# A two-layer decoder trunk on one core: a pool for layer 0's residual halves, more buffers in layer 1's attention, and spatial gating two groups to a PSUM bank

## The chip, the core and the metric

The kernel runs on one core of one Trainium2 chip. The metric is device time in microseconds (us) of one execution; the time before is the median of three runs, 2185.39 us (2182.7 to 2185.51). A core has a matrix engine (TensorE, PE in the profile; its weight loads are shown as PEld), VectorE (DVE), ScalarE (ACT), GpSimd (POOL) and SyncE (SP). Every DMA of this kernel is issued from SP's queue, in order: an issue that has to wait for something holds up the issues behind it. Matrix results land in PSUM, eight banks of 128 partitions by 512 f32 numbers; everything else stands in SBUF, 128 partitions wide.

## The reference

The input is one sequence of 1024 tokens with 1024 features, and two layers follow. Every layer is a mixer and a gated MLP, each added to the residual. Cut to what the change touches:

```python
# layer 0, mixer A: spatial gating, 8 groups of 64 columns, chunks of 128 tokens
vn = layer_norm(gelu(v), ln_g, ln_b)                 # (chunks, 128, 8, 64)
mixed = einsum('gts,bnsgc->bntgc', tril(w_s), vn) + b_s.T[:, :, None]
a_out = gelu(u) * mixed
# mixer B: dilated sliding-window attention, three branches mixed by their log-denominators -> b_out
x = x + concat([a_out, b_out]) @ w_out               # out_proj of layer 0
x = x + conv_ffn(rms_norm(x), ...)

# layer 1: gated linear attention, 4 heads, q, k 128 wide, v 256 wide
attn = where(causal, q_t @ k_t.T, 0)
o = attn @ v + q_t @ state                           # state = decay * (state + k.T @ v), chunk by chunk
o = rms_norm(o, head_g) * silu(r)
x = x + o @ w_out
x = x + conv_ffn(rms_norm(x), ...)
```

## The kernel before

Tokens are cut into eight tiles of 128 (n = 0 to 7). Products run in a split format: a number is a rounded high part and a low part (`split`, L98 to L101, one cast on ACT and one subtraction on DVE), and three matmuls (`PASSES`) give one product. The Tile framework has a planner that takes the traced program, simulates it, and fixes the order of the instructions on each engine and of the DMA issues on SP; it also places each pool's tiles. A pool is an area of SBUF or PSUM with so many buffers for each tag; pools are stacked from the left or from the right end, and an area that an earlier pool used is taken over tile by tile (`reuse_waits="tile"`): a new tile waits for the release of the old tiles that lay at its place, and of no others.

Layer 0's mixer (`even`) has five PSUM pools, opened in the order pt (2 banks), sc (2), pj (2), po (1), tq (1). `project` and `dilated` run pair after pair of heads: scores go to sc, the transposes of the probabilities to pt, the projection to pj. `gmlp` (L587) follows. `proj512` makes one v tile per n in a pj bank; after four of them `consume` normalises the half on DVE (L612 to L619) and does spatial gating: for each of eight groups g one plain f32 matmul (L623) of `ws[:, g]` with 64 columns of four token tiles, 256 columns in all, into a bank of sc, and one DVE eviction (L624) that adds the group's bias and writes over the input columns in `mx`. `u_proj` (L630) then makes the u tiles and multiplies them into `mx` (L635). The planner runs gating beside the u matmuls.

The out_proj comes in two halves of 512 output columns. `out_first` (L432) does the first: `prep(n)` loads the tile `cat` (from `bcat` in layer 0, from `ogd` in layer 1; L1140, L1145) and `xh`, the residual half (L438), transposes eight blocks into two banks of pt (`pc`, L442) and splits them into `hq`; `out_half` (L426) accumulates 24 matmuls (`po`), adds them into `xh` (L429) and writes `xh` to `xd` (L430). After the third tile `first_sides` (L214) makes weight sums for the MLP in the tags qr, qS and qw and writes them out. These PSUM tiles stand in pools mm (3) and pt (2), opened when `even` has closed its own. `out_second` (L456) does the other half in pairs of tiles: `xt` is loaded from `xd` and `x` (L497, L498), 24 matmuls are added (L429) and written out (L430), and `norm` (L144) takes the square sum on ACT (L148), the inverse root on POOL (L140, L141), scales `xt` in place on DVE (L152) and transposes it (L162).

Layer 1 (`gla`, L837): `values` (L881) makes v (L906) and writes it to `vsd`. For each head h two streams (q with k, and r; L990) run, and `core` (L1038) goes through eight chunks n: it loads a chunk of v (L1043), multiplies k and q (`pat`, L1046), turns k (L1049), copies it on ACT (`kt`, L1051), makes the chunk's k-v product (L1052), masks on DVE (L1054), adds state and chunk products into `pog` (L1056, L1057), updates the state (L1061 to L1065), takes the square sum on ACT into `og` (L1068), scales into `og` on DVE (L1070) and writes it to `ogd` (L1071). Layer 1's `out_first` gates the transposes (L1157) with `silu(r)` (L1105) before it splits them.

In the SBUF map of the compiled kernel before, op0 takes 28 KB a partition on the right, just under `gm` (the gating's tiles), with its tags from the bottom in the order cat (2 x 2 KB), xh (2 x 2), qr (2 x 4), qS (2 x 2), qw (2 x 4). The 8 KB of the first `xt` pair begin 1.5 KB above the bottom of op0.

Of the kernel before, what the change touches and what calls it, by code (L numbers as in the profile page):

```python
# [9 lines left out]
F32 = mybir.dt.float32  # L10
# [4 lines left out]
ALU = mybir.AluOpType  # L15
# [4 lines left out]
P = 128  # L20
# [6 lines left out]
GROUPS = 8  # L27
# [28 lines left out]
def trunk(ctx: ExitStack, tc: tile.TileContext, a, out):  # L56
    nc = tc.nc
    V, A, G, T, Q = nc.vector, nc.scalar, nc.gpsimd, nc.tensor, nc.sync
# [370 lines left out]
        V.tensor_add(xh, xh, pd)  # L429
        Q.dma_start(xd[l][n][:, half * 512 : half * 512 + 512], xh)  # L430

    def out_first(l, get_cat, w, x_in, ps, pool, between, gated=None):  # L432

        def prep(n):
            c = get_cat(n)
            gate = gated and gated(n)
            xh = pool.tile([P, 512], F32, tag="xh", name=f"xh{n}")
            Q.dma_start(xh, x_in(n)[:, :512])  # L438
            for g in range(2):
                pt = ps.tile([P, 4, P], F32, tag="pt", name=f"pc{n}{g}")  # L440
                for j in range(4):
                    T.transpose(pt[:, j, :], c(2 * j + g), ident)  # L442
                dst = [hq[g][n // 4][:, i, :, (n % 4) * P : (n % 4 + 1) * P] for i in range(2)]
                split(dst, gate(g, pt) if gated else pt)
            return xh

        xh = [prep(n) for n in range(AHEAD)]
        wo = load_half(w[0], "wo0")
        for n in range(NT):
            if n + AHEAD < NT:  # L450
                xh.append(prep(n + AHEAD))
            out_half(l, 0, wo, n, ps, xh[n], "m1" if l else "mm")
            if n == 2:
                between()
# [132 lines left out]
    def gmlp(ps, gm):  # L587

        wv = load_half(a["w_vu"][0], "wv", g0)
        lnG = gm.tile([P, 512], F32, name="lnG")  # L590
        Q.dma_start(lnG, a["ln_g"].partition_broadcast(P))
        lnB = gm.tile([P, 512], F32, name="lnB")
        Q.dma_start(lnB, a["ln_b"].partition_broadcast(P))
        bs = gm.tile([P, GROUPS], F32, name="bs")
        Q.dma_start(bs, a["a_bs"])
        ws = gm.tile([P, GROUPS, P], F32, name="ws")
        Q.dma_start(ws, a["a_ws"])

        G.affine_select(out=ws, in_=ws, compare_op=ALU.is_ge, fill=0.0, base=0,
                        pattern=[[0, GROUPS], [1, P]], channel_multiplier=-1)  # L600

        def consume(n, pj):
            half, j = n // 4, n % 4
            A.activation(mx[half][:, j, :], pj, AF.Copy, scale=r0[:, n : n + 1])
            if j < 3:
                return
            ge = A.activation(flat(mx[half]), flat(mx[half]), AF.Gelu)
            if half:
                tc.keep_in_program_order(ge)
            for j in range(4):  # L610
                gv = mx[half][:, j, :]
                st = small.tile([P, 6], F32, tag="bn", name=f"bn{half}{j}")  # L612
                V.bn_stats(st, gv)
                mv = small.tile([P, 2], F32, tag="mv", name=f"mv{half}{j}")
                V.bn_aggr(mv, st)
                r = inv_rms(mv[:, 1:2], 1, 1, f"lr{half}{j}")
                V.tensor_scalar(gv, gv, mv[:, 0:1], r, op0=ALU.subtract, op1=ALU.mult)
                V.tensor_mul(gv, gv, lnG)
                V.tensor_add(gv, gv, lnB)  # L619
            for g in range(GROUPS):  # L620
                gc = mx[half][:, :, g * 64 : g * 64 + 64]
                pm = ps.tile([P, 4, 64], F32, tag="sc", name=f"pm{half}{g}")
                T.matmul(pm, ws[:, g, :], gc, start=True, stop=True)  # L623
                V.tensor_scalar(gc, pm, bs[:, g : g + 1], None, op0=ALU.add)  # L624

        mx = [gm.tile([P, 4, 512], F32, name=f"mx{h}") for h in range(2)]
        proj512(ps, wv, "pv", consume)
        return [mx[n // 4][:, n % 4, :] for n in range(NT)]

# [201 lines left out]
    def odd(ps, narrow, rl):  # L831

        with tc.tile_pool(name="T", bufs=1, reuse_waits="tile") as tp, \
                tc.tile_pool(name="gl", bufs=2, reuse_waits="tile") as gl:
            return gla(ps, narrow, gl, [tp.tile([P, 2, 4, 512], F32R, name=f"Tm{i}") for i in range(3)], rl)

    def gla(ps, narrow, gl, T3, rl):  # L837
        right = {1: hq[0][0], 2: hq[1][0], 3: hq[1][1], 4: hq[0][1], 5: T3[0], 6: T3[1], 7: T3[2]}
# [42 lines left out]
        def values():  # L881

            for i, (col, step, w) in enumerate(((0, 272, 1), (256, 256, 2), (512, 512, 1))):
                if i == 0:
                    wv = [w_ for k in range(4) for w_ in load_w(a["w_v0"][k], f"wv0{k}", 272)]
                elif i == 1:
                    wv = [w_ for k in range(2) for w_ in load_w(a["w_v1"][k], f"wv1{k}")]
                else:
                    wv = load_half(a["w_v23"], "wv2")
                for m in sorted(range(NT // (2 * w)), key=lambda m: 2 * w * m < 4):  # L890
                    pv = ps.tile([P, 2, 512], F32, tag="mm", name=f"pv{i}{m}")
                    for j in range(2 * w):
                        n = 2 * w * m + j
                        mm_tok([(pv[:, j // w, (j % w) * 256 : (j % w) * 256 + step], slice(0, step))],
                               lambda k: tok(n, k),
                               lambda k: at(wv, k // 2, (k % 2) * step, step) if i == 1 else wv[k], KD)
                    end = gl.tile([P, 2, S], F32, tag="out", name="vend", bufs=1) if (i, m) == (2, 1) else None
                    for j in range(2):
                        n = w * (2 * m + j)
                        if end is not None:  # L900
                            v = end[:, j, :512]
                        elif i == 0:
                            v = gl.tile([P, 256], F32, tag="v", name=f"v{i}{n}", bufs=3)
                        else:
                            v = gl.tile([P, 512], F32, tag="s1", name=f"v{i}{n}", bufs=1)
                        A.copy(v, pv[:, j, : v.shape[-1]])  # L906
                        c = v.shape[-1] // w
                        Q.dma_start(vsd.rearrange("(n p) c -> p n c", p=P)[:, n : n + w, col : col + c],
                                    v.rearrange("p (n c) -> p n c", c=c))
                    if i == 0:  # L910
                        ns = slice(2 * m, 2 * m + 2)
                        split([gae[:, ns, 0:16], gae[:, ns, 32:48]], pv[:, :, 256:272])
                        V.tensor_copy(gae[:, ns, 64:80], f32(gae[:, ns, 0:16]))
                    if i:
                        if 2 * (i - 1) + m in [1, 0, 4, 5]:
                            three_sides([1, 0, 4, 5].index(2 * (i - 1) + m))
                    if (i, m) == (1, 1):
                        decay_input()
                    if (i, m) == (2, 2):
                        first = decays(0, "mm")  # L920
            return first
# [116 lines left out]
        def core(h, q, k, dec):  # L1038
            st = None
            for n in range(NT):  # L1040
                ts_ = slice(n * P, n * P + P)
                v = gl.tile([P, 256], F32, tag="v", name=f"v{h}{n}", bufs=3)
                Q.dma_start(v, vsd[ts_, h * 256 : h * 256 + 256])  # L1043
                three = ps.tile([P, 512], F32, tag="pt", name=f"pat{h}{n}")
                pat, pkt, pkv = three[:, :P], three[:, P : 2 * P], three[:, 2 * P :]
# [12 lines left out]
                if n < NT - 1:  # L1058
# [4 lines left out]
                        V.tensor_add(new, st, pkv)  # L1063
                    st = new
                    V.tensor_scalar(st, st, dec[:, n : n + 1], None, op0=ALU.mult)  # L1065
                og = gl.tile([P, 256], F32, tag="og", name=f"og{h}{n}")
                ssq = small.tile([P, 1], F32, tag="ssq", name=f"oss{h}{n}")
                A.activation(og, po, AF.Square, accum_out=ssq)  # L1068
                r = inv_rms(ssq, 1, 256, f"ro{h}{n}")
# [4 lines left out]
        ps = narrow()  # L1074
# [54 lines left out]
    ps = banks(pss, mm=3, pt=2)  # L1129
    for l in range(2):  # L1130
        w_out = a["od_w_out" if l else "ev_w_out"]
        x_in = (lambda n: x2[n]) if l else (lambda n: rows(a["x"], n))
        with ExitStack() as ops:
            if l == 1:
                ps, last = odd(ps, narrow, ops.enter_context(tc.tile_pool(name="rl", bufs=1, side="right", reuse_waits="tile")))
            pool = ops.enter_context(tc.tile_pool(name=f"op{l}", bufs=2, side="left" if l else "right", reuse_waits="tile"))

            def cat0(n):
# [20 lines left out]

                return gate  # L1160

            out_first(l, cat1 if l else cat0, w_out, x_in, ps, pool, lambda: first_sides(l, pool, 2), gated if l else None)
        gms.close()
        with tc.tile_pool(name=f"T{l}", bufs=1, reuse_waits="tile") as tp:
            T3 = [tp.tile([P, 2, 4, 512], F32R, name=f"T{l}{i}") for i in range(3)]
            if l == 0:
                ps = narrow()
# [4 lines left out]
        ps = banks(pss, mm=3, pt=2)  # L1172
        with ExitStack() as st:
            pool = st.enter_context(tc.tile_pool(name=f"fd{l}", bufs=1, reuse_waits="tile"))
# [103 lines left out]
```

## Time and profile before

| what | value |
|---|---|
| median of the three runs | 2185.39 us |
| profiled execution | 2186.67 us, of which the span from first to last instruction is 2185.0 us |
| PE busy | 2145.9 us, 98% of the span |
| DVE, ACT, POOL busy | 1538.2, 1032.7, 488.4 us |
| mean granted TensorE clock | 0.996 |
| DMA | 349.59 MB, mean 160 GB/s |

A page gives, for the one profiled execution, the busy time of each engine, the busy share in 40 slices, the DMA queues, the chain of work that ended last, and groups of instructions by source line. Tiles stand as out<-in by the names of the program without numbers. Four more views are used below: the busy time of each engine in given stretches; the waits (engine, line, what ended the wait, total us, how often, the longest); the timeline (start, duration, engine, line, operation, tiles, count, and in brackets the idle time before it with what ended it); and the list of one tile's or one line's instructions. A matmul's duration is that of a pipelined instruction, so a busy PE isn't a PE at its peak, and rows of several instructions are merged.

### The profile page before, as it was taken

What the parts mean: (1) busy time and instruction counts of PE and PEld (TensorE: products, weight loads), DVE (VectorE), ACT (ScalarE), POOL (GpSimd) and SP (SyncE); (2) the same over time, 40 slices, a digit from 0 to 9 for tenths busy, and PEclk for the clock granted to TensorE, in tenths of its full rate; (3) what the DMA queues carried; (4) which work ended last, traced back from release to release, by engine and by line L of the source; (5) the groups of instructions that cost most, each with busy time, mean ns of one, the idle gap of its engine ahead of it and who ended that gap; (6) DMA issues with size and microseconds to landing.
All of it is one profiled execution on the core that took longest, in us unless ns stands there. A gap on an engine that the chain in (4) does not pass through costs nothing.

```text
span 2185.0 us, 29867 instructions
## 1 busy us (share of the span) xinstructions
PE 2145.9 (98%) x10508; PEld 1817.9 (83%) x10508; DVE 1538.2 (70%) x2459; ACT 1032.7 (47%) x1998; POOL 488.4 (22%) x519
## 2 busy tenths in 40 slices
PE   8999999999999999999999999999999999999999
PEld 7999988778888888888889887878788888888887
DVE  6566655567888888755576777666787879885554
ACT  6455545355444444444454455524544444444443
POOL 4444411013242434100010011100233524320000
PEclk9999999999999999999999999999999999999999
DMA  4122212655445444675553222377544444557555
GB/s 162 43 81 63 73 50 83 217 198 194 162 155 164 158 165 159 196 271 198 196 202 123 68 97 97 116 265 248 193 160 150 158 159 159 164 178 271 204 196 202
DMA packets 157254, 349.59 MB, mean 160 GB/s; under 512 B 17408, under 2 KB 54272, under 8 KB 156720
## 3 DMA queue, kind: packets, MB, share of 16 engines
q1 hardware_dynamic: 157104, 347.68, 47.5%
q8 instruction: 83, 1.36, 0.3%
q14 instruction: 67, 0.55, 0.1%
HBM read 239.02 MB, written 108.59 MB: 159 GB/s over the span
## 4 chain that ended last, share of the span: by engine, by line
PE 70%; DMA 4%; DVE 3%; ACT 1%; issue 1%; SPq 0%; POOL 0%; DVEq 0%; ACTq 0%
PE puB L290 11%; PE pgB L290 11%; PE pgC L290 5%; PE puC L290 5%; PE pdB L397 5%; PE pdC L397 5%; PE pv L190 4%; PE pdO L397 4%; PE puA L290 3%; PE pgA L290 3%; PE po L190 2%; PE pdQ L397 2%; PE pdP L397 2%; PE pBq L990 2%; PE pBr L990 2%
## 5 line engine op out<-in xcount | busy, mean ns | idle before, releaser
L101 DVE TENSOR_TENSOR da<-ar,da 128x512 fp32r<-128x512 f32 x154 | 106.4, 691 | 155.3 <-ACT da L100 155.2
L100 ACT CAST da<-ar 128x512 fp32r<-128x512 f32 x154 | 95.9, 622 | 209.4 <-PE pdC L397 91.3
L190 PE MATMUL po<-wo,hq 128*128 128x512 f32 x768 | 186.4, 398 | 0.6 <-DVE hq L101 0.3
L190 PEld LDWEIGHTS po<-wo,hq 128*128 128x128 f32 x768 | 143.3, 190 | 30.9 <-DVE hq L101 1.2
L190 PE MATMUL pv<-wv,hq 128*128 128x512 f32 (+2 forms) x768 | 139.9, 340 | 2.1 <-DVE b L1022 1.6
L397 PE MATMUL pdB<-dw,da 128*128 128x512 f32 x528 | 136.3, 391 | 0.6 <-ACT dw L100 0.6
L397 PE MATMUL pdC<-dw,da 128*128 128x512 f32 x528 | 135.9, 390 | 0.0
L190 PEld LDWEIGHTS pv<-wv,hq 128*128 128x128 f32 x768 | 119.0, 189 | 17.4 <-DVE b L1022 2.1
L190 PE MATMUL pj<-wq,hq 128*128 128x384 f32 x576 | 118.1, 348 | 0.0
L397 PEld LDWEIGHTS pdB<-dw,da 128*128 128x128 f32 x528 | 98.7, 188 | 21.9 <-ACT dw L100 1.0
L397 PEld LDWEIGHTS pdC<-dw,da 128*128 128x128 f32 x528 | 99.1, 188 | 20.4
L256 POOL TENSOR_TENSOR S1g<-rg 128x512 f32<-128x512 f32 x20 | 29.6, 1480 | 381.2 <-DMA wsd<-D 326.9
L101 DVE TENSOR_TENSOR dw<-wr,dw 128x512 fp32r<-128x512 f32 x154 | 105.9, 687 | 11.2 <-ACT dw L100 11.1
L140 POOL TENSOR_SCALAR rn<-ssq 128x1 f32<-128x1 f32 x24 | 8.1, 337 | 470.1 <-ACT h L148 245.6
L397 PE MATMUL pdO<-dw,da 128*128 128x512 f32 x396 | 102.3, 390 | 0.2 <-DVE dw L101 0.2
L100 ACT CAST dw<-wr 128x512 fp32r<-128x512 f32 x154 | 95.0, 617 | 15.0 <-DMA wr<-in_w_dn 7.6
L190 PEld LDWEIGHTS pj<-wq,hq 128*128 128x128 f32 x576 | 101.0, 192 | 0.4 <-ACT vN L718 0.2
L397 PEld LDWEIGHTS pdO<-dw,da 128*128 128x128 f32 x396 | 74.3, 188 | 15.9 <-DVE dw L101 0.6
L319 DVE SCALAR_TENSOR_TENSOR t<-g,cw,t 128x1022 f32<-128x1022 f32 x44 | 76.7, 1742 | 0.1
L318 DVE SCALAR_TENSOR_TENSOR t<-g,cw,t 128x1023 f32<-128x1023 f32 x44 | 59.4, 1350 | 16.5 <-ACT t L317 16.5
L303 DVE TENSOR_TENSOR g<-g,s1g 128x512 f32<-128x512 f32 x22 | 16.2, 738 | 77.1 <-ACT s1g L302 77.1
L320 ACT ACTIVATE t<-t 128x1024 f32<-128x1024 f32 x44 | 46.7, 1061 | 32.7 <-DVE t L319 32.7
(1073 smaller groups left out, 5478.7 us busy)
## 6 DMA issues: line engine op xcount, KB each, us to landing
ar<-actd SPq DMA_DIRECT2D x70, 512.0 KB, 3.5
rd<-in_w_down SPq DMA_DIRECT2D x44, 512.0 KB, 3.6
wsd<-D SPq DMA_DIRECT2D x88, 256.0 KB, 2.4
rg<-in_w_gate SPq DMA_DIRECT2D x42, 512.0 KB, 3.6
ru<-in_w_up SPq DMA_DIRECT2D x42, 512.0 KB, 4.8
wr<-wsd SPq DMA_DIRECT2D x40, 512.0 KB, 4.4
actd<-t SPq DMA_DIRECT2D x66, 256.0 KB, 2.2
wr<-in_w_dn SPq DMA_DIRECT2D x30, 512.0 KB, 4.9
```

Source lines behind the costliest of these rows:

```text
L100: (hi or A.copy)(dst[0], src)
L101: (lo or V.tensor_sub)(dst[1], src, f32(dst[0]))
L140: G.tensor_scalar(r, ssq, 1.0 / n, EPS, op0=ALU.mult, op1=ALU.add)
L190: T.matmul(o, L[i], R[jj][:, sl], start=(k == 0 and (ii, jj) == PASSES[0]), stop=(k == nk - 1 and (ii, jj) == PASSES[-1]))
L256: G.tensor_tensor(sums[name], x, y, op=op)
L290: T.matmul(o, L[ii][:, j * P : j * P + P], right[p][:, jj, j, :], skip_group_check=more, start=(not more and j == 0 and (ii, jj) == PASSES ...
L303: V.tensor_add(C22, C22, s1)
L318: V.scalar_tensor_tensor(t[:, 1:], g[:, : S - 1], w(1), t[:, 1:], op0=ALU.mult, op1=ALU.add)
L319: V.scalar_tensor_tensor(t[:, 2:], g[:, : S - 2], w(0), t[:, 2:], op0=ALU.mult, op1=ALU.add)
L320: A.activation(t, t, AF.Silu)
L397: T.matmul(o, L[ii][:, t * P : t * P + P], R[jj], skip_group_check=more, start=start and not more and (ii, jj) == PASSES[0], stop=stop and ...
L990: T.matmul(o, L[ii][:, j * P : j * P + P], right[p][:, jj, j, :], skip_group_check=more, start=(not more and j == 0 and (ii, jj) == PASSES ...
```

## The change

There are three edits. First, the residual halves `xh` of layer 0's `out_first` come from a pool of their own, `xhp`, with two buffers as before, opened on the right ahead of op0; layer 1 keeps `xh` in its pool. Second, in layer 1 the tag `v` goes from 3 to 6 buffers and `og` from 2 to 4. Third, spatial gating takes its PSUM tiles from pt and not from sc, puts two groups into one bank (two matmuls of 256 columns, side by side), and evicts both with one DVE addition of 512 columns whose bias is broadcast from `bs`.

```diff
-    def out_first(l, get_cat, w, x_in, ps, pool, between, gated=None):
+    def out_first(l, get_cat, w, x_in, ps, pool, between, gated=None, xhp=None):
...
-            xh = pool.tile([P, 512], F32, tag="xh", name=f"xh{n}")
+            xh = (xhp or pool).tile([P, 512], F32, tag="xh", name=f"xh{n}")
...
-            for g in range(GROUPS):
-                gc = mx[half][:, :, g * 64 : g * 64 + 64]
-                pm = ps.tile([P, 4, 64], F32, tag="sc", name=f"pm{half}{g}")
-                T.matmul(pm, ws[:, g, :], gc, start=True, stop=True)
-                V.tensor_scalar(gc, pm, bs[:, g : g + 1], None, op0=ALU.add)
+            for g in range(0, GROUPS, 2):
+                pm = ps.tile([P, 2, 4, 64], F32, tag="pt", name=f"pm{half}{g}")
+                for i in range(2):
+                    T.matmul(pm[:, i], ws[:, g + i, :], mx[half][:, :, (g + i) * 64 : (g + i) * 64 + 64],
+                             start=True, stop=True)
+                V.tensor_tensor(mx[half][:, :, g * 64 : g * 64 + 128].rearrange("p n (i c) -> p i n c", i=2), pm,
+                                bs[:, g : g + 2, None, None].to_broadcast([P, 2, 4, 64]), op=ALU.add)
...
-                            v = gl.tile([P, 256], F32, tag="v", name=f"v{i}{n}", bufs=3)
+                            v = gl.tile([P, 256], F32, tag="v", name=f"v{i}{n}", bufs=6)
...
-                v = gl.tile([P, 256], F32, tag="v", name=f"v{h}{n}", bufs=3)
+                v = gl.tile([P, 256], F32, tag="v", name=f"v{h}{n}", bufs=6)
...
-                og = gl.tile([P, 256], F32, tag="og", name=f"og{h}{n}")
+                og = gl.tile([P, 256], F32, tag="og", bufs=4, name=f"og{h}{n}")
...
+            xhp = None if l else ops.enter_context(tc.tile_pool(name="xhp", bufs=2, side="right", reuse_waits="tile"))
             pool = ops.enter_context(tc.tile_pool(name=f"op{l}", bufs=2, side="left" if l else "right", reuse_waits="tile"))
...
-            out_first(l, cat1 if l else cat0, w_out, x_in, ps, pool, lambda: first_sides(l, pool, 2), gated if l else None)
+            out_first(l, cat1 if l else cat0, w_out, x_in, ps, pool, lambda: first_sides(l, pool, 2), gated if l else None, xhp)
```

## The prediction

> **What bounds the kernel now.** I read the head of the page first, then the busy time by stage (columns: stretch, its length, busy time and count of PE, PEld, DVE, ACT and POOL, granted clock, DMA share, GB/s).
>
> ```profile
> span 2185.0 us, 29867 instructions
> ...
> PE 2145.9 (98%) x10508; PEld 1817.9 (83%) x10508; DVE 1538.2 (70%) x2459; ACT 1032.7 (47%) x1998; POOL 488.4 (22%) x519
> ```
>
> ```profile
> 348.00:392.00 44.00, 41.42 (x195) 33.92 (x194) 24.37 (x54) 15.85 (x24) 2.60 (x2) 1.00 0.40 124
> 392.00:500.00 108.00, 104.93 (x507) 87.17 (x506) 66.33 (x106) 46.22 (x98) 7.76 (x16) 0.98 0.61 208
> 500.00:916.00 416.00, 415.08 (x1833) 343.08 (x1832) 348.16 (x378) 194.66 (x316) 146.32 (x80) 1.00 0.50 164
> ...
> 1230.00:1440.00 210.00, 205.23 (x942) 169.23 (x941) 142.97 (x287) 106.59 (x222) 30.84 (x67) 1.00 0.32 104
> 1440.00:1560.00 120.00, 115.27 (x557) 94.16 (x556) 85.30 (x148) 54.52 (x114) 7.84 (x16) 0.99 0.78 265
> ```
>
> TensorE is the bound: 2185.0 - 2145.9 = 39 us idle in all, and in the gate and up projections (500 to 916) under 1 us. What the change touches lies in four stretches: spatial gating beside the u projection (348 to 392, 2.6 us idle), layer 0's out_proj (392 to 500, 3.1), the attention core of layer 1 (1230 to 1440, 4.8) and the start of its out_proj (1440 to 1560, 4.7): 15 us. No edit removes a large matmul, so almost all that can be won is idle time there. The view of waits, for PE, names it (total, times, longest):
>
> ```profile
> PE pc L442 <- DMA cat<-ogd: 3.1, 2, 2.5
> PE pat L1052 <- DMA v<-vsd: 2.7, 4, 1.2
> ...
> PE pt L162 <- DVE xt L152: 2.3, 1, 2.3
> ...
> PE pc L442 <- DVE hq L101: 1.7, 1, 1.7
> ...
> PE pCr L990 <- ACT or L1000: 1.1, 1, 1.1
> ...
> PE pc L442 <- DVE mx L624: 0.7, 1, 0.7
> ...
> PE pCr L990 <- DVE og L1070: 0.5, 1, 0.5
> ```
>
> **Part 1: residual halves in their own pool.** op0 and its neighbours stand on the right of SBUF. Before, the tags of op0 lie in the order cat, xh, qr, qS, qw, 28 KB in all; the 8 KB of xt00, the first tile of out_second, begin 1.5 KB above its bottom and so lie on cat, both xh buffers and the start of qr. Hence this stretch (waits of SP, then the timeline, whose columns are start, duration, what, count, idle before):
>
> ```profile
> SPq L497 <- DMA xd<-xh: 4.6, 1, 4.6
> ```
>
> ```profile
> 441.43 0.69 DVE L101 TENSOR_TENSOR qw0u<-qu,qw0u 128x512 fp32r<-128x512 f32 x1
> ...
> 444.78 0.42 SPq L430 DMA_DIRECT2D xd<-xh  x1
> ...
> 445.75 0.33 SPq L110 DMA_DIRECT2D rg<-in_w_gate  x1
> ...
> 450.76 0.33 SPq L497 DMA_DIRECT2D xt<-xd  x1
> ...
> 455.33 0.69 DVE L429 TENSOR_TENSOR xt<-xt,po 128x512 f32<-128x512 f32 x1 [9.61 <-DMA xt<-in_x]
> ...
> 456.04 0.33 SPq L430 DMA_DIRECT2D xd<-xt  x1
> ...
> 460.93 1.65 DVE L152 TENSOR_SCALAR xt<-xt,rn 128x1024 f32<-128x1024 f32 x2 [3.38 <-DMA xd<-xt]
> ...
> 461.74 2.70 PE L162 MATMUL pt<-ident,xt 128*128 128x128 f32 x12 [2.34 <-DVE xt L152]
> ```
>
> The load of xt waits 4.6 us for the last xh to be written out, although it needs no number from it. From there a chain runs: load, add at 455.33, write-out, in-place scaling at 460.93 (it overwrites what is being written out), transposes at 461.74 with PE idle 2.3 us. After the change the total stays 28 KB, but xh lies above op0, and xt00 lies on cat and qr, which are read for the last time at 442.1 (L101 at 441.43). Even if SP keeps its order, the loads leave at 446.1 instead of 450.8 and the chain ends 4.6 us earlier, at about 456.3 + 0.8: twice the 2.3 us that PE lacks. What is late next there is the matmul stream itself. Cost of the move: the xh buffers now lie under the fourth temporary and two of the 2 KB temporaries of out_second; these are first written after the add (455.33, or 450.7 when it comes 4.6 us earlier), and xh is out by 450.7. Gain: 2.3 us.
>
> **Part 2: spatial gating, two groups a bank.** The matmul count stays at 16 (32 instructions); 16 evictions of 256 columns become 8 of 512, with a bias broadcast. Groups and lines of before:
>
> ```profile
> L623 PE MATMUL pm<-mx,ws 128*128 128x256 f32 x32 | 9.6, 381 | 0.0
> L624 DVE TENSOR_SCALAR mx<-pm,bs 128x256 f32<-128x256 f32 x16 | 7.7, 482 | 19.1 <-PE pm L623 19.0
> ```
>
> ```profile
> L470 DVE TENSOR_TENSOR n<-pt,gT x8: 681/686/692, 463.1 to 495.9; 128x512 f32<-128x512 f32 x8
> ```
>
> L470 is the same form as the new eviction (PSUM in, a broadcast operand, 512 columns). DVE: 8 x 0.686 = 5.5 us for 7.7; the 2.2 us lie beside the matmuls and are counted at nothing. On PE there are two terms.
>
> ```profile
> 374.01 0.60 PE L623 MATMUL pm<-mx,ws 128*128 128x256 f32 x2
> ...
> 374.25 2.42 PE L190 MATMUL pu<-wu,hq 128*128 128x512 f32 x9
> ...
> 376.51 0.60 PE L623 MATMUL pm<-mx,ws 128*128 128x256 f32 x2
> ...
> 377.90 0.43 SPq L1140 DMA_DIRECT2D cat<-bcat  x1
> ...
> 387.06 2.50 DVE L635 TENSOR_TENSOR mx<-mx,ut 128x512 f32<-128x512 f32 x4
> ...
> 387.08 0.44 PE L442 MATMUL pc<-ident,mx 128*128 128x128 f32 x2 [0.67 <-DVE mx L624]
> ...
> 390.82 0.44 PE L442 MATMUL pc<-ident,mx 128*128 128x128 f32 x2 [1.67 <-DVE hq L101]
> ```
>
> ```profile
> 532.25 2.72 PE puB L290 x12
> ```
>
> (the last is from the chain of waits). Undisturbed matmuls of 512 columns start every 2.72 / 12 = 0.227 us. The nine after a pm take 2.42; nine in a plain run take 8 x 0.227 + 0.39 (the 390 ns of one, as in the page's groups) = 2.21. So each return from the f32 gating matmul costs 0.2 us. Eight returns instead of sixteen save 8 x 0.2 = 1.6 us. Bounds: nothing, if the planner splits the pairs, and 1.6; I take 1.6, the nearest row.
>
> The other term is the hand-over to out_proj. The five PSUM pools of layer 0's mixer lie in the order pt (banks 0, 1), sc (2, 3), pj (4, 5), po, tq; the pools that follow put their five tiles on banks 0 to 4, and the transposes pc fall on banks 3 and 4. Bank 3 belonged to sc, which the last pm held until its eviction (L624) was done: that is the 0.67 us. Then DVE does four products and only afterwards the split that frees pc: 1.67 us. After the change pm lies in pt, bank 3 has been free since the last scores, and the transposes of tile 0 can run beside the last u matmuls. The first out_proj accumulator (bank 0) now inherits pm's bank, but with half as many turns through two banks the gating should end well before the u projection does. Of 0.7 + 1.7 I take 2.2, and leave 0.2 for what else the first accumulation waits for (the split of wo).
>
> [...]
>
> **Part 3: buffers of layer 1's core.** Six v buffers and four og buffers, with nothing else in the pool's way (5 KB more, in a gap of 15 KB between the left and right pools). Waits of SP and of ACT:
>
> ```profile
> SPq L1043 <- PE pat L1049: 43.3, 16, 10.7
> ```
>
> ```profile
> ACT og L1068 <- DMA ogd<-og: 19.0, 9, 3.3
> ```
>
> Before, the load of v waits in SP's queue for a buffer, 43.3 us in all, and SP issues nothing else meanwhile. With six, the loads of chunks 3 to 5 don't wait on the head's own chunks, and chunks 6 and 7 go out when 0 and 1 are done, some 5 chunks ahead of use. PE's 2.7 us for v goes. With four og buffers ACT no longer stops at L1068 for the write-out (19.0 us), and what stands behind it in ACT's queue comes earlier: kt, and the evictions that free the banks for which PE waits 1.1 and 0.5 us. Together 1.6; I take 1.3.
>
> The 3.1 us for cat I leave. The stretch after it shows why:
>
> ```profile
> 1440.80 0.58 ACT L1004 COPY or<-pBr 128x512 f32<-128x512 f32 x1 [0.94 <-PE pBr L990]
> ...
> 1441.81 1.06 ACT L1105 ACTIVATE or<-or 128x1024 f32<-128x1024 f32 x1
> ...
> 1443.58 0.60 DVE L1157 SCALAR_TENSOR_TENSOR gt<-pc,hg,or 128x128 f32<-128x128 f32 x2
> ...
> 1445.34 12.55 PE L190 MATMUL po<-wo,hq 128*128 128x512 f32 x48
> ```
>
> Even with cat there, the product needs the last stream's silu (1441.81 + 1.06) and the accumulation starts only after product and split: the gate is late next.
>
> **The sum.** 2.3 + 1.6 + 2.2 + 2.7 + 1.3 = 10.1 us. The planner lays out all queues anew, and where v is no longer late the chain from chunk to chunk may be; for this I give back 1.5 us, a choice between 0 and the 4 us of idle time that would make the v and og gain void. Net 8.6. The profiled execution took 2186.67 (its span 2185.0 and 1.7 around it), giving 2178.1; the median of the runs shown, 2185.39, is 1.3 lower, so I forecast **2177**.
>
> **The rivals.**
> - *Little comes of it.* The static orders have other tight places: a wait that goes is followed by the next (kt, the silu gate, the write-out before L152). For: the cat wait above, and that the stalls are single waits of 1 to 2 us, which a DMA some us later makes again. Against: part 1 has 4.6 us of slack for 2.3. If half of the waits return and the switches stay, 10.1 becomes 3: 2182 to 2184.
> - *The paired bank stalls PE* (the side of a slower kernel). In pt, gating now shares two banks with the transposes of the last dilated units. If PE's fixed order has pm ahead of them, each of eight pm banks can show its round trip, at least the 0.60 us of the matmuls and the 0.69 of the eviction: 8 x 1.3 = 10.3 us. And four banks at the pace of now (374.01 to 376.51, 2.5 us each) put the units' results 10 us back. Their way goes on through bcat to cat, issued at 377.90; with 4.9 us to land, as the write-out from 456.04 to 460.93, that leaves 4.3 us before the transposes at 387.08, so 5.7 us of PE idle there. 10.3 + 5.7 less the 6.3 of parts 1 and 3 is 9.7 us slower: 2195. It makes the kernel slower from the point where these stalls exceed 6.3 us. Against: the planner takes earlier parts of the program first, and there are filling matmuls. [...]
> - *The pools do not do what they say*: xt still waits, now for qr or for SP's place in the queue. Then only 2.3 is missing: 2179; it lies within the forecast.
>
> **Chances.** Forecast (with the last case) 0.70; little 0.16; paired bank or another order that hurts 0.14. What can be told from no change here is about 0.2%, 4.4 us: faster means under 2181.0, slower over 2189.8. So faster 0.70, same 0.17, slower 0.13. The range: down to all the waits named (2.3 + 2.4 + 1.6 + 2.7 + 1.6 + 3.1 = 13.7) from 2185.4, and 2.7 us more for SP's freed queue, 2169; up through the second case to 2190, where half of the slower one begins.
>
> **What would show it.** Part 1: the SP wait for xd<-xh and PE's wait at L162 gone. Part 2: eight evictions of about 0.69 us, gating ended before 380, no wait of pc at L442 on DVE around 387. Part 3: no PE wait for v, ACT's 19 us for ogd gone, the cat wait still there. I am wrong if idle time in these four stretches stays near 15 us, if PE idles between 340 and 360, or if stretches that are full now (500 to 916) open gaps.

## The result and the profile after

The changed kernel takes 2178.82 us (median of 8, 2175.36 to 2180.23) where the kernel before takes 2185.56 us (8, 2182.7 to 2192.71) on the same chip: ratio 0.9957, 95% interval 0.9945 to 0.9969: 6.7 us between the medians, 9.4 by the ratio (which is not the quotient of the two medians; that would be 0.9969). The forecast was 2177. The profiled execution of the change took 2178.69 us. Its page begins, and its busy time by stage reads (columns as in the prediction; each stage is the one shown there, moved to where the work now lies):

```profile
span 2176.9 us, 29864 instructions
...
PE 2139.8 (98%) x10508; PEld 1812.1 (83%) x10508; DVE 1534.4 (70%) x2451; ACT 1034.1 (48%) x1998; POOL 490.8 (23%) x519
```

```profile
345.00:389.00 44.00, 42.84 (x208) 35.62 (x207) 22.81 (x49) 17.95 (x29) 2.60 (x2) 1.00 0.33 96
389.00:497.00 108.00, 104.94 (x515) 86.56 (x515) 66.66 (x107) 47.61 (x100) 8.59 (x16) 1.00 0.63 218
497.00:912.00 415.00, 414.17 (x1829) 342.19 (x1828) 347.30 (x378) 194.07 (x314) 146.58 (x80) 1.00 0.50 163
1226.00:1434.00 208.00, 205.19 (x946) 169.84 (x946) 143.50 (x289) 108.63 (x223) 29.52 (x67) 1.00 0.33 106
1434.00:1553.00 119.00, 114.32 (x560) 93.53 (x559) 85.80 (x150) 55.70 (x116) 8.83 (x16) 1.00 0.78 267
```

The first thing to see is where the 8.1 us between the two spans (2185.0 and 2176.9) do *not* come from. TensorE runs the same 10508 matmuls, yet its busy time is 6.1 us less (2145.9 to 2139.8), and its idle time only 2.0 us less (39.1 to 37.1). In the four stages of the change idle time fell from 15.2 us to 1.2 + 3.1 + 2.8 + 4.7 = 11.7. So in the whole span more of the gain is busy time than idle time. Of the 6.1 us, 1.4 lie before the first u matmul, where idle time rose by 1.2 us and the change touches nothing. Another part is matmuls that ran faster, as the next two views show: the same stretch of the first xt transposes and of the first out_proj matmuls of layer 1, in the kernel before

```profile
462.00:466.00 4.00, 4.00 (x18) 3.68 (x17) 2.44 (x5) 2.69 (x7) 0.74 (x2) 0.58 0.17 66
1445.00:1449.00 4.00, 4.00 (x14) 3.29 (x13) 3.77 (x8) 1.34 (x3) 0.00 (x0) 0.58 1.03 406
```

and in the changed one:

```profile
459.00:464.00 5.00, 4.42 (x26) 3.88 (x27) 3.38 (x6) 2.70 (x7) 0.74 (x2) 1.00 0.14 52
1437.00:1441.00 4.00, 4.00 (x20) 3.01 (x21) 3.57 (x9) 1.96 (x4) 0.00 (x0) 1.00 1.04 404
```

The column after POOL is the granted clock: 0.58 before, 1.00 after, so 14 matmuls fit into 4 us there and 20 here. By the trace's clock records TensorE ran at half clock from 461.9 and from 1444.9 us, 3.4 us each, in the kernel before; the changed kernel has no such window between 31 us and its end. By busy time each costs 1.2 to 1.3 us in this pair: TensorE is busy 93.4 us in out_proj before and 92.2 after, and 39.9 and 38.6 us at the start of layer 1's out_proj. The first came behind the 2.3 us wait at L162, the second behind a 2.5 us wait for cat.

The waits of PE in the changed kernel, of those that the prediction speaks of:

```profile
PE pc L442 <- DMA cat<-ogd: 2.6, 3, 1.3
PE pBq L992 <- ACT oq L1000: 2.1, 2, 1.1
...
PE pt L162 <- DVE xt L152: 1.5, 1, 1.5
...
PE po L190 <- ACT hq L100: 1.0, 1, 1.0
...
PE pCr L992 <- ACT or L1002: 0.7, 1, 0.7
...
PE pc L442 <- DVE hq L101: 0.2, 1, 0.2
```

Lines behind the gating loop have moved by two (L990 is L992, L1052 is L1054). Gone are the 2.7 us for v and the 0.7 us at L442 for mx; 1.7 us at L442 for hq became 0.2, but the first accumulation waits 1.0 (L190), and pBq, 0.5 us before, waits 2.1. SP's wait of L497 fell from 4.6 us to this row:

```profile
SPq L497 <- DMA xd<-xh: 0.3, 1, 0.3
```

Yet the xt chain did not come 4.6 us earlier. Its timeline after the change:

```profile
444.45 0.33 SPq L110 DMA_DIRECT2D rg<-in_w_gate  x1
444.87 0.50 SPq L497 DMA_DIRECT2D xt<-xd  x1
445.42 0.48 SPq L498 DMA_DIRECT2D xt<-in_x  x1
...
454.13 0.69 DVE L429 TENSOR_TENSOR xt<-xt,po 128x512 f32<-128x512 f32 x1 [9.71 <-DMA xt<-in_x]
...
458.77 1.58 DVE L152 TENSOR_SCALAR xt<-xt,rn 128x1024 f32<-128x1024 f32 x2 [2.62 <-DMA xd<-xt]
...
459.58 1.53 PE L162 MATMUL pt<-ident,xt 128*128 128x128 f32 x12 [1.48 <-DVE xt L152]
```

The load left 5.9 us earlier than in the kernel before (444.87 and 450.76), but the add began only 1.2 us earlier (454.13 and 455.33): what the load won in SP's queue it lost in flight. The hand-over to out_proj, and the new evictions (the list of line L625):

```profile
387.87 0.73 PE L190 MATMUL po<-wo,hq 128*128 128x512 f32 x2 [0.96 <-ACT hq L100]
388.80 0.44 PE L442 MATMUL pc<-ident,mx 128*128 128x128 f32 x2 [0.20 <-DVE hq L101]
```

```profile
L625 DVE TENSOR_TENSOR mx<-pm,bs x8: 679/691/693, 352.7 to 376.7; 128x512 f32<-128x512 f32 x8
```

Clock windows come and go between executions (the kernel before has them at 461.9 and 1444.9 us, and in neither place when it ran again, e8), and the eight runs of the change alone lie 4.9 us apart, so whole spans are poor evidence below 5 us. So I cut every profiled execution at the start of the same six TensorE instructions: the first u matmul, the 33rd out_proj matmul, the second gate matmul of the feed-forward, the first core matmul of layer 1 (pAq), the first cat transpose of layer 1 and the 520th out_proj matmul. The time to the first of them, 323 to 330 us in these executions, lies before anything that the change touches. The lengths between, in us, from the timelines of all kernels of this study:

| kernel | u to out_proj | out_proj | to core | core | layer 1 start | xt wait | v waits | longest cat wait | half-clock windows from 340 to 1560 |
|---|---|---|---|---|---|---|---|---|---|
| before | 71.8 | 96.5 | 738.7 | 206.0 | 43.3 | 2.3 | 2.7 | 2.5 | 461.9, 1444.9 |
| before again (e8) | 71.8 | 95.3 | 739.4 | 203.1 | 41.0 | 1.8 | 0.3 | 1.6 | none |
| pool only (e1) | 73.5 | 94.2 | 739.7 | 205.8 | 41.8 | 0.5 | 1.8 | 1.9 | 388.3 |
| gating only (e2) | 70.0 | 95.2 | 742.0 | 205.0 | 42.1 | 2.0 | 0.9 | 1.9 | 941.4 |
| buffers only (e3) | 71.8 | 96.3 | 739.1 | 202.8 | 41.1 | 2.3 | 0 | 1.2 | 464.0 |
| bank only (e4) | 80.5 | 97.6 | 739.3 | 206.1 | 43.1 | 3.2 | 2.3 | 2.1 | 384.9 (13.7 us), 470.2, 1453.3 |
| pairs in sc (e7) | 70.1 | 95.3 | 741.9 | 204.0 | 44.2 | 2.0 | 1.3 | 3.4 | 1193.4, 1442.6 |
| without pool (e11) | 70.0 | 100.3 | 740.3 | 202.9 | 41.5 | 5.4 | 0 | 1.5 | 459.3 (6.8 us) |
| without gating (e12) | 71.8 | 94.3 | 739.5 | 202.8 | 41.2 | 0.6 | 0 | 1.4 | none |
| the change | 70.0 | 95.3 | 739.0 | 202.8 | 41.5 | 1.5 | 0 | 1.3 | none |
| the change again (e5) | 70.0 | 94.1 | 740.9 | 202.9 | 40.9 | 0.5 | 0 | 1.2 | none |
| xt first (e6) | 70.0 | 93.9 | 743.1 | 202.8 | 43.1 | 0 | 0 | 2.0 | 1453.6 |
| scale apart (e9) | 70.0 | 99.9 | 739.2 | 202.9 | 41.6 | 2.0 | 0 | 1.6 | 460.1 |
| both (e10) | 70.0 | 94.6 | 739.2 | 203.1 | 41.6 | 0 | 0 | 1.2 | none |

(The xt wait is the longest single wait at the first transposes of xt, L162 or L161, without later tiles; the v waits are a total; the others are as in the rows of waits. A wait just before one of the six instructions counts to the stage that this instruction ends.)

### The profile page after: what moved, and what is told of

The parts are those of the page before. It is cut to its first block, busy times and chain, and to the rows that moved or that the text cites. A ratio compares the mean times of both kernels' runs of the same rounds, so it can differ in the third digit from the quotient of the medians.

```text
span 2176.9 us, 29864 instructions
## 1 busy us (share of the span) xinstructions
PE 2139.8 (98%) x10508; PEld 1812.1 (83%) x10508; DVE 1534.4 (70%) x2451; ACT 1034.1 (48%) x1998; POOL 490.8 (23%) x519
## 4 chain that ended last, share of the span: by engine, by line
PE 87%; DMA 5%; DVE 3%; ACT 3%; issue 1%; POOL 0%; SPq 0%; DVEq 0%; ACTq 0%; POOLq 0%
PE puB L290 11%; PE pgB L290 11%; PE pv L190 6%; PE pj L190 6%; PE pgC L290 5%; PE puC L290 5%; PE pdB L397 5%; PE pdC L397 5%; PE pdO L397 4%; PE po L190 3%; PE puA L290 3%; PE pgA L290 3%; PE pdQ L397 2%; PE pdP L397 2%; PE pu L190 2%; PE pBq L992 2%
## 5 line engine op out<-in xcount | busy, mean ns | idle before, releaser
L190 PE MATMUL po<-wo,hq 128*128 128x512 f32 x768 | 184.4, 395 | 1.6 <-ACT hq L100 1.0
L190 PEld LDWEIGHTS po<-wo,hq 128*128 128x128 f32 x768 | 141.6, 188 | 31.7 <-ACT hq L100 1.4
L190 PE MATMUL pv<-wv,hq 128*128 128x512 f32 (+2 forms) x768 | 139.8, 339 | 2.1 <-DVE b L1024 1.6
L190 PEld LDWEIGHTS pv<-wv,hq 128*128 128x128 f32 x768 | 119.0, 189 | 17.4 <-DVE b L1024 2.1
L190 PE MATMUL pj<-wq,hq 128*128 128x384 f32 x576 | 116.2, 343 | 0.2 <-ACT vN L720 0.2
L190 PEld LDWEIGHTS pj<-wq,hq 128*128 128x128 f32 x576 | 99.2, 189 | 0.5 <-ACT vN L720 0.4
```

Of the source, the lines that this page charges most:

```text
L190: T.matmul(o, L[i], R[jj][:, sl], start=(k == 0 and (ii, jj) == PASSES[0]), stop=(k == nk - 1 and (ii, jj) == PASSES[-1]))
```

## The experiments

The first theory was the prediction's: each part takes away its own waits, and the waits are the gain. Its rivals: the parts only work together; a gain is given back at the next wait; part of the gain is the clock.

**e1, e2, e3: one part alone.** The edits are the three parts of the diff as shown.

> Only the pool of layer 0's residual halves; the rest as before. My accounting of the two traces: the xt loads leave some 4.5 us earlier than before against the matmul stream but land hardly earlier, because weight loads ahead of them fill the DMA engines; PE's wait at L162 falls from 2.3 to about 1.5 us, and the half-clock window of 3.4 us at 462 goes or stays by chance: 0.8 us faster, 2.2 with the window gone, so 2183 to 2185 against 2185.6. The prediction's own step (chain 4.6 us earlier, wait gone) would give 2.3 us and an add (L429) at about 450.7. A rival: the gain in this stretch comes from the earlier parts of the change and the pool alone does nothing: 0.

> Only the spatial gating (two groups a bank, in pt). From the two traces: 0.9 us for the wait of pc on L624, 0.3 in the u stretch, 0.6 in the rest of the hand-over: 1.8 us faster, about 2183.8. The prediction had 3.8 (1.6 for fewer returns from the f32 matmul, 2.2 for the hand-over): 2181.8. If the rival of the shared bank held, PE would wait between 340 and 380 and the kernel were slower.

> Only six v buffers and four og buffers. From the two traces: 2.7 us of v waits and 0.5 of og gone, 1.6 given back to waits of pBq on ACT, and at the start of layer 1's out_proj the waits shorter by 0.9 and a half-clock window of 3.4 us gone (1.5 us): 4 to 5 us faster, about 2181. The prediction had 4.0 for the core and nothing for the out_proj. If the clock window is what the tail gained by, the clock records show none near 1440.

Measured, beside 2184.72 us before: 2183.8 (ratio 0.9991, 0.998 to 1.0001), 2182.09 (0.999, 0.998 to 1.0001) and 2183.41 (0.9994, 0.9981 to 1.0007). None alone can be told from no change; added, they are 0.25%. For e3, 4 to 5 us had been expected, and 1.3 us lie between the medians. In its profile the core and the start of layer 1's out_proj take 5.4 us less than in the first execution of the kernel before, from which the 4 to 5 us were worked out, but only 0.2 us less than in e8, which has no change at all. By stage each does its work in its own place: pool only 94.2 in out_proj, gating only 70.0 at the hand-over, buffers only 202.8 in the core. In e1 the window at 462 is gone, but another, at 388, makes the hand-over 1.7 us longer (73.5). Of the buffers' gain a part is handed to the query projection at once, as the waits of e3 show (0.5 us in the kernel before):

```profile
PE pBq L990 <- ACT oq L998: 2.1, 2, 1.1
```

**e4: one group per bank, but in pt.** It tells the pairing from the move.

```
-                pm = ps.tile([P, 4, 64], F32, tag="sc", name=f"pm{half}{g}")
+                pm = ps.tile([P, 4, 64], F32, tag="pt", name=f"pm{half}{g}")
```

> Gating keeps one group a bank and 256-column evictions, but takes its banks from pt. If the move of the bank brings part 2's gain and the pairing nothing, this gives the same 1.8 us as the gating alone (about 2183.8) and pc no longer waits for L624. If the pairing brings it (fewer returns from the f32 matmul, fewer evictions), this stays at 2185.6, with the last eviction still near 387.

Measured: 2194.71 us, ratio 1.0045 (1.0029 to 1.006), slower, and 8.7 us of it at the hand-over (80.5 for 71.8). Its timeline there:

```profile
380.54 1.03 PE L623 MATMUL pm<-mx,ws 128*128 128x256 f32 x4
...
387.11 3.21 PE L623 MATMUL pm<-mx,ws 128*128 128x256 f32 x6 [4.18 <-DVE mx L624]
393.21 1.12 PE L442 MATMUL pc<-ident,cat 128*128 128x128 f32 x4 [2.89 <-DMA cat<-bcat]
```

Sixteen turns through two banks shared with the dilated units last until after the u projection is used up (pm at 387), the units' results reach cat late (2.9 us), and from 384.9 us on, 2.0 us into the wait that ends at 387.11, TensorE has half clock (0.50, the column before the last two):

```profile
388.00:392.00 4.00, 2.32 (x5) 0.88 (x4) 3.13 (x7) 0.00 (x0) 0.00 (x0) 0.50 1.02 348
```

That is the mechanism of the prediction's slower rival, in the kernel that has the move without the pairing: 4.2 us for the round trip and 2.9 for cat, where the rival had 10.3 and 5.7. Of the 8.7 us, idle time is 4.7 (7.3 for 2.6) and busy time 4.0 (73.2 for 69.2, at half clock from 384.9 us on).

**e7: pairs, but left in sc.** `tag="pt"` of the changed gating loop is `tag="sc"`, and nothing else of the change is in.

> Two gating groups per bank with eight 512-wide evictions, but in the banks of sc, as before. Theory A (pairing alone wins nothing on TensorE, since the gain of part 2 is the hand-over of bank 3): ratio 1.000, and PE still waits for a DVE result at L442 near 387, 0.5 to 2.4 us in all. Rival (fewer returns from the f32 matmul save 0.2 us each, as the prediction has it): 1.6 us, ratio 0.9993, also where the wait at L442 stays. Rival C (with half as many turns gating ends some us before the u projection, so bank 3 is free in time in either place): the wait is gone too, and the ratio is that of part 2 alone, 0.999.

Measured: 2183.63 us beside 2186.1, ratio 0.9987 (0.9973 to 1.0002). The hand-over in its timeline:

```profile
376.64 7.87 PE L190 MATMUL pu<-wu,hq 128*128 128x512 f32 x34
...
386.35 0.73 PE L190 MATMUL po<-wo,hq 128*128 128x512 f32 x2 [0.96 <-ACT hq L100]
387.28 0.44 PE L442 MATMUL pc<-ident,mx 128*128 128x128 f32 x2 [0.21 <-DVE hq L101]
```

These are the changed kernel's own waits (0.96 and 0.20), and the stage takes 70.1. Its last rival holds: gating with half as many turns ends early enough that bank 3 is free in either place (the last eviction starts at 370.0 us here and the first transpose for out_proj at 384.35). The pairing is part 2's gain; the move to pt brings nothing.

**e5 and e8: the change and the kernel before once more, unchanged.**

> The whole change once more, beside single parts on the same chip. Theory A (the three parts add up): its gain is the sum of the single parts, 0.09 + 0.10 + 0.06 = 0.25%, so ratio 0.9975, about 2180.2 us at 2185.6 before. Theory B (the parts need each other, since TensorE has no room to keep what one part alone wins): ratio 0.9957 as in the first comparison, 2176 to 2179. On the clock: if the half-clock windows follow the kernel, the profile shows them again at about 24 us and at the end only; if they follow the execution, they lie elsewhere, and the stretch from 0 to 144 us then differs by 1.5 us or more from the first profile of the same kernel.

> The kernel before, unchanged, for a second profile of the same program. Theory A (the half-clock windows of 3.4 us follow the execution): they are not at 45, 69, 462 and 1445 us again, and the stretches that contained one are 1.4 to 1.6 us shorter, above all the start of layer 1's out_proj (1440 to 1450). Rival (they follow the program's own idle spells): they appear at the same places, to within a few us.

Measured: the change 2176.39 us, ratio 0.9957 (0.9942 to 0.9971); the one run of the kernel before 2183.09. The windows at the start of the change lie at 45 and 69 us, not at 24, so they follow the execution. And the kernel before, run again, has neither the window at 462 nor that at 1445:

```profile
462.00:466.00 4.00, 2.22 (x17) 2.04 (x17) 2.70 (x4) 0.74 (x1) 0.14 (x1) 1.00 0.23 81
1443.00:1447.00 4.00, 4.00 (x20) 3.12 (x19) 3.91 (x8) 1.58 (x3) 0.00 (x0) 1.00 1.02 396
```

Its waits in these places were shorter too:

```profile
PE pc L442 <- DMA cat<-ogd: 2.7, 2, 1.6
...
PE pat L1052 <- DMA v<-vsd: 0.3, 1, 0.3
```

Each run also has a mean granted clock. Over 28 runs of the kernel before and 11 of the change, on the same chip, it averages 0.9970 and 0.9986. With TensorE taken as busy throughout, 0.0016 of 2185 us is 3.5 us, of the 9.7 between these medians: by this estimate about a third of the gain is the clock. It is a rough one, as the runs scatter by 0.0014 and 0.0012.

From the first u matmul to the 520th out_proj matmul the execution of e8 needs 1150.6 us, the first one of that kernel 1156.3, the change 1148.7 and 1148.8. So an execution of the kernel before can come within 2 us of the change over these stages. The first one lost the other 5.7 us in longer waits (v, cat) and in the two windows behind such waits.

**e6: the xt loads ahead of the weights.** On top of the change, the raw gate and up weights are issued after the first pair of xt loads.

```
+            with tc.issue_after(xt_loads[-1]):
+                raws = [load_raw(w_of(kind)[l, f + i], f"r{kind}{f + i}") for i in range(2 if f else 1)]
...
+                ins = Q.dma_start(xt[:, 512:], x_in(n)[:, 512:])
+                if l == 0 and i == 0:
+                    xt_loads.append(ins.ins)
```

> The whole change, and the raw gate and up weight loads of out_second's start are issued after the first two xt loads of layer 0. Theory A (the xt loads land late because they queue behind 512 KB of weights at about 400 GB/s): the first half of x lands about 4 us after its issue instead of 8.6, the add at L429 begins at about 450 instead of 454, and PE's wait of 1.5 us for the scaled xt at L162 is gone: 1 to 1.5 us faster than the change (ratio to it 0.9993 to 0.9995). Rival (PE's own stream is next, the wait goes but the time does not): no wait at L162, ratio 1.000. Rival C: the weights come too late for the gate projection, and PE waits there (L290) for 1 to 4 us: slower than the change by that.

Measured: 2181.78 us, ratio to before 0.9977 (0.9964 to 0.9991), where the change has 0.9957 on the same chip: the 1 to 1.5 us gain did not come. The rows of SP's queue and DVE:

```profile
441.79 0.43 SPq L501 DMA_DIRECT2D xt<-in_x  x1
...
488.79 0.33 SPq L433 DMA_DIRECT2D xd<-xt  x1
```

```profile
446.21 0.69 DVE L432 TENSOR_TENSOR xt<-xt,po 128x512 f32<-128x512 f32 x1 [4.09 <-DMA xt<-in_x]
...
495.64 0.75 DVE L152 TENSOR_SCALAR xt<-xt,rn 128x1024 f32<-128x1024 f32 x1 [4.29 <-DMA xd<-xt]
```

Theory A is right about the loads: the first tile's half of x lands 4.4 us after its issue instead of 8.7, the wait at L162 is gone, and out_proj takes 93.9 us. But the next stage takes 743.1 instead of 739.0 to 740.9. TensorE waits 5.1 us around its first gate products, where the change waits 1.3 and 0.2:

```profile
PE pgB L293 <- DVE hq L101: 2.4, 1, 2.4
PE puA L293 <- DVE g L299: 1.2, 1, 1.2
PE pgC L293 <- DVE T L101: 1.0, 1, 1.0
PE pgB L293 <- ACT T L100: 0.5, 1, 0.5
```

The first ends at 489.4, with the second gate matmul: it is for the split of an earlier tile, and it was 1.3 us in the change. The other three come behind the last tile. Its write-out leaves at 488.79, the in-place scaling waits for it and starts 6.9 us later, and DVE's work for these products stands in the queue behind the scaling. Rival C gave about the right size and the right place, but it named the weights; what is late is the last tile.

**e9 and e10: the scaling into another tile.** The chain from xt to the transposes should not wait for a write-out. Both kernels drop one line of `norm`; e10 has the edit of e6 as well.

```
         if gB is None:
-            h = xt
             V.tensor_scalar(h, xt, r, None, op0=ALU.mult)
```

In both, the second four transposes of a tile read blocks that the first eviction has already overwritten in part, and they wait for that eviction: so this part of the computation is another one, and there is a round trip per tile which the change has not. (Rival C of e9 has this wait the other way round.)

> The whole change, and the scaling before out_second's transposes writes into the tile that holds the squares instead of over xt, which is still being written out. Theory A (after the change the write-out of xt is what is late: 1.5 us at L162 and, behind the last tile, 1.3 us at L290): both PE waits go, 1.5 to 2.8 us faster than the change, ratio to before 0.9944 to 0.9950 where the change has 0.9957. Rival (the loads are late and nothing else): DVE stops waiting for the write-out, but its add waits for x as before, and the ratio stays at 0.9957. Rival C (the first eviction now has to wait for all eight transposes of a tile, since they read the tile that it writes): TensorE waits for banks, slower than the change by up to 8 tiles of 0.3 us, 0.9968.

> e6 and e9 together. Theory A (what e6 won by earlier loads, 2 us, it gave back because the scaling of the last tile waited 4.3 us for its write-out): with that wait gone the 2 us stay, ratio to before at most that of e9, near 0.9945. Rival (the weights that now come later, or the order of DVE's queue, make TensorE wait in the first gate products): PE waits at L293 of 2 us and more remain, and the ratio stays near e6's 0.9977.

Measured: e9 2183.64 us, ratio 0.9985 (0.9974 to 0.9996); e10 2179.86, ratio 0.9963 (0.9952 to 0.9975), both beside 2187.86. e9 loses some 5 us in out_proj against the change: its waits there hold the new round trip, and the first transposes still wait, for another chain. Its timeline:

```profile
455.13 0.69 DVE L428 TENSOR_TENSOR xt<-xt,po 128x512 f32<-128x512 f32 x1 [9.32 <-DMA xt<-in_x]
455.90 1.06 ACT L148 ACTIVATE n<-xt 128x1024 f32<-128x1024 f32 x1 [12.07 <-DVE xt L428]
...
457.41 0.55 POOL L141 TENSOR_TENSOR rn<-rn,mhalf 128x1 f32<-128x1 f32 x1
457.99 0.75 DVE L151 TENSOR_SCALAR n<-xt,rn 128x1024 f32<-128x1024 f32 x1 [2.18 <-DMA xd<-xt]
```

L151 starts at 457.99, when POOL's 0.55 us from 457.41 are over; the DMA in its bracket (xd<-xt) is not what it waits for, since it no longer writes what is being written out. From the start of the add to the scaling it is now 2.9 us (4.6 in the change), but the load is late as before, so 2.0 us of wait remain, with a half-clock window behind them (at 460.1 us). In e10 both causes are gone. The last tile's scaling carries no wait, and no wait is left in the first gate products (L292, which is L293 in e6):

```profile
492.45 0.75 DVE L151 TENSOR_SCALAR n<-xt,rn 128x1024 f32<-128x1024 f32 x1
```

The stage to the core takes 739.2 us again, where e6 had 743.1. So e6's gain went into waits for write-outs before the scaling. e10's time can't be told from the change's (0.9963 and 0.9957), as the round trip stays in it; a version that keeps the values and has no round trip was not tried, and no kernel here is shown to beat the change.

**e11 and e12: the change without one part.** The pool, or the gating loop, as before.

> The change without part 1 (xh stays in op0's pool). Theory A (the parts add up): 0.09% slower than the whole, ratio to before 0.9966. Theory B (the parts need each other): more than 0.2% slower than the whole, 0.9977 or above. On the profile: SP's wait of about 4.6 us for xd<-xh is back, and the xt loads leave about 5 us later than in the whole change, in both theories.

> The change without part 2 (gating one group per bank, in sc). Theory A (the parts add up): 0.10% slower than the whole, ratio to before 0.9967. Theory B (the parts need each other): 0.9978 or above. On the profile: the waits of about 0.7 and 1.7 us at L442 near 387 are back in both theories, and TensorE's lead against before at the first out_proj accumulation is 0, not 2 us, once the start's differences are taken off.

Measured: 2181.7 us, ratio 0.9973 (0.9957 to 0.9988), and 2178.63, ratio 0.9959 (0.9944 to 0.9974). For gating theory B falls: 0.9978 lies outside. For the pool the interval holds both 0.9966 and 0.9977. Each wait is back where it was expected; without the pool the one at L162 is 5.4 us, more than in any other kernel, and the half-clock window there is 6.8 us long instead of 3.4 (SP's waits, PE's timeline and the busy time of that stretch):

```profile
SPq L497 <- DMA xd<-xh: 6.2, 1, 6.2
```

```profile
461.44 2.82 PE L162 MATMUL pt<-ident,xt 128*128 128x128 f32 x12 [5.42 <-DVE xt L152]
```

```profile
460.00:464.00 4.00, 2.56 (x13) 2.56 (x13) 2.70 (x4) 1.12 (x3) 0.00 (x0) 0.50 0.13 46
```

## Why the prediction was right, and which of its terms were not

**The whole** is right: 2177.0 forecast, 2178.82 and 2176.39 measured, 8.6 us forecast against the profiled execution and 8.0 found. The stages of the pair add up as 0.2 before the first u matmul + 1.8 + 1.2 - 0.3 + 3.2 + 1.8 + 0.2 = 8.1 us of span. Several terms were mis-sized, and they cancelled; and no term was for the clock, which by the estimate above is about a third of the gain. That the total came so near is in part luck.

**Part 1, 2.3 forecast, 0.8 to 2 found.** That the load's wait for xd<-xh goes was right (4.6 to 0.3 us). "The loads leave at 446.1 and the chain ends 4.6 us earlier" failed in its second half: with three weight loads ahead of it in the queue the first tile's half of x took 8.7 us from its issue to the add instead of 4.2 (451.14 to 455.33 in the kernel before), and e6, with the loads ahead of the weights, shows 4.4. Without a clock window out_proj takes 94.1 to 95.3 us with the pool (mean of the change, e5, e1 and e12: 94.5) and 95.2 or 95.3 without it (e8, e2, e7): 0.8 us. The first execution before and e3 have the window and take 96.5 and 96.3: 1.9 us. In e11 it is 5.8 us.

**Part 2, 3.8 forecast, 1.8 found.** The hand-over was right in kind. The waits of the kernel before there, 0.7 + 1.7 + 0.2, became 1.0 + 0.2: 1.4 of the 2.2. The transposes of tile 0 did not move beside the u matmuls, as I had written; TensorE's order puts them behind, and what is late next is the split of hq on ACT. The reason with the banks was not needed: e7 has the same gain in sc. The 1.6 us for "each return from the f32 gating matmul costs 0.2 us" is the step that failed. In the timeline of the changed kernel the pm matmuls stand in only 6 groups, two of eight and four of four, where the kernel before has 16 groups of two. They show what a return costs:

```profile
363.06 1.89 PE L623 MATMUL pm<-mx,ws 128*128 128x256 f32 x8
364.60 4.68 PE L190 MATMUL pu<-wu,hq 128*128 128x512 f32 x19
369.12 1.03 PE L623 MATMUL pm<-mx,ws 128*128 128x256 f32 x4
```

From 363.06 to 369.12 are 6.06 us; 19 u matmuls at 0.227 us are 4.31, so eight pm matmuls cost 1.75 us, 0.22 each. In the prediction's rows, from 374.01 to 376.51 are 2.50 us; nine u matmuls are 2.04, so two pm matmuls cost 0.46 us, 0.23 each. In these rows the cost goes with the number of pm matmuls, which stays at 32, and hardly with the number of returns: 0.22 us each in a turn of eight, 0.23 each in a turn of two. By this count the extra time in the u matmuls behind a pm row belongs to the pm matmuls: in the prediction's rows the u matmuls start 0.24 us after two pm matmuls (374.01 to 374.25), which cost 0.46.

**Part 3, 4.0 forecast with 1.5 given back; 3.2 found in this pair, 2.2 on average.** With the buffers the core takes 202.8 to 203.1 us in eight executions of eight. Without them it takes 203.1 to 206.1 in six, and the longest are those with most waiting for v. Their mean is 205.0, so 2.2 us. Not all of it is idle time: TensorE is busy 200.0 or 200.1 us of the core with the buffers and 200.9 to 201.6 without, with no window in either, and no run shows why. The 1.5 us given back in the sum has a name: pBq waits 2.1 or 2.2 us for oq in all eight kernels with the buffers, 0.5 in the kernel before. Of the og term the 0.5 us for og came; the wait for or fell from 1.1 to 0.7, which e8 has as well. ACT's 19.0 us at L1068 are gone, as forecast. SP's wait for a v buffer is not: it fell from 43.3 us in 16 waits to 36.9 in 8, so the loads go out ahead of need, but the queue is hardly freer. Six v buffers without four og buffers weren't tried.

**The cat wait, left at 0.** Its total barely moved (3.1 to 2.6), as forecast, but its longest single wait fell from 2.5 to 1.3, and with it a window: the start of layer 1's out_proj took 1.8 us less. This gain was in no term. e8 had it with no change at all.

**The rivals.** "Little comes of it" is out, since 0.9957 came twice. The paired bank does not stall; the bank alone does (e4, 8.7 us at the place named, where I had 16). That was a neighbour of the change, and the pairing is what keeps the change from it: e7 and the change take 70.1 and 70.0 us at this place, 71.8 before, with u matmuls to fill the round trips (0.0 us idle before the pm matmuls), and e4, with one group per bank through two banks, takes 80.5.

What stays open: whether the gains of the parts only add up, and how much of the whole is the clock. The single parts give 0.25% and the whole 0.43% (0.31 to 0.55 in the first comparison), and a single part's interval is a tenth of a per cent or more either way. By stages they add up; whether the pool's part is worth more in company (e11) is one execution.

## What to carry to other kernels

Cut two profiles at the same instructions and compare stage by stage, with the granted clock beside it: a busy TensorE may be a slow one (granted clock 0.58 at 462 and at 1445 us in the kernel before), and there the 2.3 us wait at L162 with a window behind it cost about 3.5 (2.3 idle and 1.2 of busy time). A load that left 5.9 us earlier, but behind three others, arrived only 1.2 us earlier, so ask of each released transfer what is in flight then. And after a win, look for the next chain with the same form (here the last tile's write-out), because it may take back more than was won.

## What the runs showed of the hardware

The clock was not expected to matter on one core that is 98% busy. At the xt transposes of layer 0 a half-clock window comes with every single wait of 2.3 us and more (2.3 in before and e3, 3.2 in e4, 5.4 in e11) and with none of 2.0 us or less in seven others (e8, e2, e7, the change, e5, e1, e12); e9, with 2.0, is the exception. At layer 1's cat one comes with each of 2.0 us and more (2.5 in before, 2.1 in e4, 2.0 in e6, 3.4 in e7) and with none up to 1.9. The windows of the table last 3.4 us, in two cases longer (6.8 in e11, 13.7 in e4), and in the one at 1444.9 in the kernel before a matmul of 512 columns takes its turn every 0.427 us (po, 1445.9 to 1448.0) instead of 0.227 (from 1448.4 on). At 388.3 in e1 one follows two waits of 0.7 and 1.7 us which bring none in the kernel before, e8, e3 or e12, so the length of the wait does not decide alone. Elsewhere the pattern fails: the clock stays at 1.00 behind a wait of 3.0 us at 24.8 in e9, of 2.6 us at 24.3 in e4 and of 2.4 us at 489.4 in e6. No run varied a wait alone, so this is a pattern of 14 executions at two places and not an experiment of its own, and no run shows what sets the clock.
